# A hybrid attention trunk on one core: the third product of a unit without a follower in a PSUM bank of its own, VectorE adding the second sum to it in place of ScalarE's copy

## The chip, the core and the metric

The kernel runs on one core of one Trainium2 chip. A core has a matrix engine (TensorE, PE in the profile; PEld is its loading of weights), VectorE (DVE), ScalarE (ACT), GpSimd (POOL) and SyncE (SP), which issues most DMAs. TensorE writes only to PSUM, of which this kernel uses eight banks; VectorE and ScalarE read them out. Each engine works through its own queue in order, and waits for other engines on semaphores. The metric is device time in microseconds (us), lower is better.

## The reference

16 learned meta tokens are put ahead of 512 tokens of width 1024. Then come two layers, each with a pre-norm, a combined input projection, a branch, a SiLU gate and an output projection that is added to the stream; a final norm drops the meta tokens.

```python
def reference(x, meta, g_norm, ..., g_final):
    h = jnp.concatenate([meta, x], axis=1)              # 528 tokens x 1024, float32
    h = h + gla_branch(rmsnorm(h, g_norm[0]), ...)      # 4 heads, gated linear attention
    h = h + diff_branch(rmsnorm(h, g_norm[1]), ...)     # 8 heads, differential softmax attention
    return rmsnorm(h[:, 16:], g_final)

def gla_branch(xn, w_in, ...):
    q, k, v, z, g_lr = jnp.split(xn @ w_in, [...], axis=-1)
    ...                                  # causal, with a decay for each key channel
    return (silu(z) * head_rms(o) * gnorm) @ w_out

def diff_branch(xn, w_in, ...):
    q, k, v, z = jnp.split(xn @ w_in, 4, axis=-1)
    a = softmax(q1 k1 + bias) - lam * softmax(q2 k2 + bias)
    return (silu(z) * head_rms(a @ v) * gnorm * ...) @ w_out
```

## The kernel before

Activations lie transposed, channels on the 128 partitions and tokens along the free dimension, in two halves of 264 tokens (256 where the meta tokens are left out). Float32 accuracy is had from a faster matmul format by splitting each operand into a high part (ScalarE copies it, L276) and a low remainder (VectorE subtracts, L277): names that end in h and l, such as wh and wl. Three of the four cross products of the parts are summed.

Most input projections are done by a `Unit`: a 1024x256 block of weights is cut into quarters and multiplied with both token halves in Strassen's manner, with seven products where eight would be usual. A product is 12 matmuls into one PSUM bank (`PASSES`, L431). The banks bv and by exist once, bx twice, and a new tile named bx takes the other bx bank in turn. Sums and differences of the products become the four quarters of the result:

- The first product goes into a bx bank, and ScalarE copies it out as u (`partial`, L452; call it u1). The unit before can do this ahead of time (`nxt.first()`), so that the next starts early (`early`).
- The second product adds to the same bank, and ScalarE copies the sum out as u2.
- The third product adds to the same bank again, and ScalarE copies the sum out as u3.
- The fifth product goes into bv. VectorE makes one quarter from bv and u3 (L477), and then the sixth product adds to bv.
- The product in by and u1 make a quarter (L479), the fourth product and u3 make another (L477), and bv with u2 make the last (L479).

For a unit that was started early and has no other Unit behind it (`early and not nxt`, the only case that the change touches) TensorE's order is: second product (`p6` in the code), fifth (`p5`, bv), third (`p7`), the by product (`p2`), fourth (`p4`, bx), sixth (`p3`, bv); where `freed` is set the fourth stands right behind the third.

TensorE's order is written out by the code itself: a `Weaver` takes a few matmuls at a time from a queue of generators and places them between the steps of the attention. The other engines' queues are set by a scheduler: it takes what the code issues, by priorities (`urgent`, `soon`, `at_once`) and by its own notion of when an input will be there. So an instruction that is replaced can also reorder its neighbours on ScalarE and VectorE.

Other names that occur: in the first layer `kd` (decayed keys) is scaled on VectorE (L1218) between groups of matmuls (L1214), and `cm`, `c` are splits of those scores; `vm` is the short block of values of a head, written in three parts from a DMA's `lands` (L407 and L408 on ScalarE, L412 on VectorE) and used by L1244; L934 and L935 are a gate's tanh and its scaling, L936 the product on VectorE; `tick` is a small memset that releases the copies of v (L575); L1253 squares an output row, L972 is the output projection and L980 adds it to the stream. In the second layer `aT` and `am` are splits of transposed attention weights (L276, L277, L407, L408, L410), and L1723 multiplies `am` with the short block of values; L1740 makes a gated row `yt`, which is split into `y`.

Of the kernel before, what the change touches and what calls it, by code (L numbers as in the profile page):

```python
# [11 lines left out]
F32 = mybir.dt.float32  # L12
# [4 lines left out]
ALU = mybir.AluOpType  # L17
# [3 lines left out]
P = 128  # L21
# [7 lines left out]
HT = L // 2  # L29
# [180 lines left out]
def trunk(ctx, tc, x, meta, g_norm, gla_w_in, gla_w_gate_up, gla_b_gate, gla_gnorm, gla_w_out,  # L210
# [3 lines left out]
    act, dve, pe, pool, sp = nc.scalar, nc.vector, nc.tensor, nc.gpsimd, nc.sync  # L214
# [17 lines left out]
    def T(p, shape, dt, tag, **kw):  # L232
        uid[0] += 1
        return p.tile(shape, dt, tag=tag, name=f"{tag}_{uid[0]}", **kw)

    def pb_tile(tag):
        return T(pb_pool, [P, 512], F32, tag, bufs=2 if tag == "bx" else 1)
# [75 lines left out]
    def load(key):  # L313
        t = load_w(*key) if len(key) == 4 else load_blocks(*key)
        while behind:
            behind.pop(0)[0]()
        for i in spare.pop(key[1:], ()):
            residual_rows(i)
        return t
# [10 lines left out]
    ws = Weights(lambda *key: load(key), {"pair": 2, "sum": 1, "a11": 1, "a12": 1, "a22": 1})  # L330
# [56 lines left out]
    def want_plain(w, c0, keep=False):  # L387

        def first(raw):
            with behind_gate():  # L390
                return block_pair(raw[:, :8, :], keep)

        return ws.want((w, c0, True), [Part("pair", first),
                                       Part("pair", lambda raw: block_pair(raw[:, 8:, :]))])
# [33 lines left out]
    def product(bank, w, x, first=True):  # L428

        for i, (k, p, q) in enumerate(PASSES):  # L430
            pe.matmul(bank[:, :x[q].shape[2]], w[p][:, k * P:(k + 1) * P], x[q][:, k, :], start=first and i == 0,  # L431
                      stop=i == len(PASSES) - 1, skip_group_check=not first)
            if i % 3 == 2:
                yield 0.33

    class Unit:
# [13 lines left out]
        def partial(self):  # L450
            t = T(up[0], [P, HT], F32, "u", bufs=3)[:, :self.n]
            W.moved = act.activation(t, self.bx[:, :self.n], AF.Copy, scale=self.sc)  # L452
            return t

        def first(self):
            a11 = self.u[0]
            w = ws.use(a11)
            self.bx = pb_tile(self.tags[0])
            yield from product(self.bx, w, self.X["b11"])
            ws.done(a11)  # L460
            self.p1 = self.partial()

        def run(self):
            X, sc = self.X, self.sc
            a11, a12, a22, s21, s43 = self.u
            early = self.bx is not None
            nxt = W.following()
            nxt = nxt if isinstance(nxt, Unit) else None
            out = []

            @at_once
            def add(i, n, bank, t, sign):
                if not out:
                    out.extend(o if isinstance(o, list) else [o[:, :self.n], o[:, self.n:]] for o in self.dst())
                o, bank = out[i][n], bank[:, :self.n]
                if sign < 0:
                    W.mark = dve.scalar_tensor_tensor(o, bank, -sc, t, op0=ALU.mult, op1=ALU.subtract)  # L477
                elif sc == 1.0:
                    W.mark = dve.tensor_tensor(o, bank, t, op=ALU.add)  # L479
                else:  # L480
                    W.mark = dve.scalar_tensor_tensor(o, bank, sc, t, op0=ALU.mult, op1=ALU.add)

            def p2():
                by = pb_tile(self.tags[1])
                yield from product(by, ws.use(a12), X["b21"])
                ws.done(a12)
                add(0, 0, by, self.p1, 1)

            def p4():
                bz = pb_tile("by" if nxt else "bx")  # L490
                yield from product(bz, ws.use(a22), X["t4"])
                ws.done(a22)
                add(1, 0, bz, self.u3, -1)
                self.tail(1)

            def p5():
                self.bv = pb_tile("bv")
                yield from product(self.bv, ws.use(s21)[1], X["t1"])

            def p6():  # L500
                yield from product(self.bx, ws.use(s21)[0], X["t2"], False)
                self.u2 = self.partial()

            def p7():
                yield from product(self.bx, ws.use(s43)[1], X["t3"], False)
                self.u3 = self.partial()
                add(1, 1, self.bv, self.u3, -1)

            def p3():
                yield from product(self.bv, ws.use(s43)[0], X["b22"], False)  # L510
                ws.done(s43)
                add(0, 1, self.bv, self.u2, 1)
                self.tail(0)

            if not early:
                yield from self.first()
            before, after = {(True, True): ((p2, p5), ()), (True, False): ((p5,), (p2,)),
                             (False, True): ((p5,), ()), (False, False): ((p2,), ())}[early, nxt is not None]
            if not early:
                yield from (p2 if nxt else p5)()  # L520
            yield from p6()
            for f in before:
                yield from f()
            ws.done(s21)
            if self.freed:
                self.freed()
            yield from p7()
            if self.freed:
                yield from p4()
                self.freed()  # L530
            for f in after:
                yield from f()
            if nxt:
                yield from nxt.first()
            if not self.freed:
                yield from p4()
            yield from p3()
# [13 lines left out]
    def x_parts(i, pool=xp):  # L551
        t = T(pool, [P, 2, 4, HT], F32R, f"x{i}", bufs=1)
        return [t[:, j] for j in range(2)]

    X = {n: x_parts(i) for i, n in enumerate(("b11", "b21", "b22", "t1", "t2", "t4"))}
# [7 lines left out]
    up = [gctx.enter_context(tc.tile_pool(name="up", bufs=3))]  # L563
# [78 lines left out]
    for b in range(5):  # L642
        t0, n = BLK[b]
        t = T(gp, [P, D], F32, ("qs", "ks")[b - 1]) if b in (1, 2) else {0: z2, 3: v2[0], 4: v2[1]}[b][:, 1, :]
# [859 lines left out]
    X = {f"b{i + 1}{n + 1}": [t[:, :, n * HT:(n + 1) * HT] for t in B[i]] for i in range(2) for n in range(2)}  # L1504
# [440 lines left out]
def build(shapes):  # L1945
    import concourse.bacc as bacc

    nc = bacc.Bacc("TRN2", target_bir_lowering=False, num_devices=1, dynamic_dma_scratch_size=512)
    args = [nc.dram_tensor(f"in_{n}_dram", shp, F32, kind="ExternalInput").ap() for n, shp in shapes]
    args.append(nc.dram_tensor("out_0_dram", (1, NR, D), F32, kind="ExternalOutput").ap())  # L1950
    with tile.TileContext(nc) as tc:
        trunk(tc, *args)
    return nc
# [15 lines left out]
```

## Time and profile before

| | us |
|---|---|
| median of 3 runs | 971.44 (970.47 to 972.05) |
| the profiled execution | 970.65 |
| its span, first to last instruction | 968.9 |
| TensorE matmul busy | 957.2 |
| TensorE weight load busy | 906.9 |
| VectorE busy | 778.6 |
| ScalarE busy | 626.8 |
| GpSimd busy | 44.9 |

Busy times are of the span; those of different engines overlap. The clock that TensorE was granted was 0.999 of full speed over the span. A row of the timeline gives the start and the length in us, the engine, the line, the operation, the tile written and those read, the shape, and a count where equal instructions follow each other; a bracket tells of idle time ahead of it and what ended it. Matmuls overlap, so a row of TensorE is as long as its last matmul's modelled end; the starts within a product are 0.12 us apart.

### The profile page before, as it was taken

Reading aid. Unit: us, or ns where it says so; the run is one execution under the profiler, and the core shown is the slowest. Engines: PE = TensorE matmul, PEld = TensorE weight load, DVE = VectorE, ACT = ScalarE, POOL = GpSimd, SP = SyncE. Lnnn points to the kernel's source line nnn. Section 1 sums busy time; section 2 is a strip of 40 time slices with the busy share of each in tenths; the row PEclk is TensorE's granted clock in tenths of the full one; section 3 lists DMA queues with packets and bytes.
Section 4 is the critical chain, followed back from the end, with each engine's and each line's share of the span. In section 5 each row is a group of like instructions: output and inputs, shape, how many; then the busy total and the mean of one; then the engine's idle time right before and its main releaser. Section 6 shows DMA issues by size and latency. Waiting matters only on the chain.

```text
span 968.9 us, 18048 instructions
## 1 busy us (share of the span) xinstructions
PE 957.2 (99%) x6993; PEld 906.9 (94%) x6993; DVE 778.6 (80%) x1586; ACT 626.8 (65%) x1304; POOL 44.9 (5%) x68
## 2 busy tenths in 40 slices
PE   9999999999999999999999999999999999999997
PEld 8999999999999999998899998998999989989996
DVE  7989885886888787668997987968869769687785
ACT  7776755577647567656757776575675756755583
POOL 1000000000000000000001001000000000000001
PEclk9999999999999999999999999999999999999999
DMA  7322223635363236124355525243342341722212
GB/s 197 88 85 59 82 79 122 147 103 128 116 162 91 85 117 158 53 101 152 99 130 138 143 73 133 75 139 98 99 138 88 118 119 44 182 70 84 89 64 87
DMA packets 128522, 104.94 MB, mean 108 GB/s; under 512 B 51102, under 2 KB 112830, under 8 KB 128433
## 3 DMA queue, kind: packets, MB, share of 16 engines
q1 hardware_dynamic: 123104, 93.80, 35.1%
q10 hardware_dynamic: 5328, 9.95, 2.8%
q8 instruction: 56, 0.92, 0.4%
q14 instruction: 34, 0.27, 0.1%
HBM read 83.64 MB, written 11.80 MB: 99 GB/s over the span
## 4 chain that ended last, share of the span: by engine, by line
PE 88%; ACT 1%; DVE 1%; issue 1%; POOLq 0%; DVEq 0%
PE bx L431 19%; PE bv L431 12%; PE by L431 10%; PE bx L421 10%; PE ps L400 9%; PE bx L972 5%; PE bx L400 3%; PE bv L972 2%; PE by L972 2%; PE ps L1214 2%; PE by L400 2%; PE bv L400 2%; PE ps L1807 1%; PE bx L1807 1%; PE bv L421 1%; PE by L421 1%
## 5 line engine op out<-in xcount | busy, mean ns | idle before, releaser
L277 DVE TENSOR_TENSOR wl<-raw,wh 128x1024 fp32r<-128x1024 f32 x98 | 119.4, 1221 | 23.0 <-ACT wh L276 18.9
L276 ACT ACTIVATE wh<-raw 128x1024 fp32r<-128x1024 f32 x98 | 103.1, 1054 | 48.3 <-PE by L972 22.9
L431 PE MATMUL bv<-x,wh 128*128 128x264 f32 (+1 forms) x656 | 98.6, 287 | 0.0
L431 PE MATMUL bx<-x,wh 128*128 128x264 f32 (+1 forms) x640 | 95.6, 286 | 0.0
L431 PEld LDWEIGHTS bv<-x,wh 128*128 128x128 f32 x656 | 86.8, 189 | 0.6 <-DVE z L479 0.2
L431 PEld LDWEIGHTS bx<-x,wh 128*128 128x128 f32 x640 | 84.6, 188 | 0.7 <-ACT u L452 0.2
L452 ACT ACTIVATE u<-bx 128x264 f32<-128x264 f32 (+1 forms) x120 | 45.3, 379 | 35.5 <-PE bx L431 33.1
L1694 ACT ACTIVATE p<-p,st 128x528 f32<-128x528 f32 (+3 forms) x64 | 36.5, 570 | 41.7 <-DVE st L1692 41.4
L421 PE MATMUL bx<-x,wh 128*128 128x512 f32 (+1 forms) x256 | 62.4, 385 | 0.0
L277 DVE TENSOR_TENSOR wl<-sum,wh 128x1024 fp32r<-128x1024 f32 x41 | 50.1, 1221 | 10.6 <-ACT wh L276 10.5
L431 PE MATMUL bx<-x,wl 128*128 128x264 f32 (+1 forms) x320 | 54.1, 284 | 0.0
L431 PE MATMUL bv<-x,wl 128*128 128x264 f32 (+1 forms) x328 | 53.8, 284 | 0.1
L421 PEld LDWEIGHTS bx<-x,wh 128*128 128x128 f32 x256 | 44.4, 188 | 7.8
L276 ACT ACTIVATE wh<-sum 128x1024 fp32r<-128x1024 f32 x41 | 43.1, 1051 | 9.7 <-PE by L972 3.9
L431 PE MATMUL by<-x,a12h 128*128 128x264 f32 (+1 forms) x320 | 47.5, 286 | 0.1
L1730 POOL TENSOR_TENSOR st<-st,mhalf 128x1 f32<-128x1 f32 x32 | 25.5, 795 | 468.6 <-ACT on L1728 418.2
L431 PE MATMUL bx<-x,a11h 128*128 128x264 f32 (+1 forms) x320 | 46.6, 284 | 0.0
L431 PEld LDWEIGHTS bv<-x,wl 128*128 128x128 f32 x328 | 45.4, 188 | 0.3 <-issue 0.3
L431 PEld LDWEIGHTS bx<-x,wl 128*128 128x128 f32 x320 | 45.3, 188 | 0.3
L431 PEld LDWEIGHTS bx<-x,a11h 128*128 128x128 f32 x320 | 42.4, 188 | 0.6
L431 PEld LDWEIGHTS by<-x,a12h 128*128 128x128 f32 x320 | 42.1, 188 | 0.3 <-ACT t L1658 0.3
L276 ACT ACTIVATE a11h<-raw 128x512 fp32r<-128x512 f32 x41 | 25.7, 626 | 20.7 <-DMA raw<-in_diff_w_in_dram 7.9
(493 smaller groups left out, 2631.9 us busy)
## 6 DMA issues: line engine op xcount, KB each, us to landing
raw<-in_gla_w_in_dram SPq DMA_DIRECT2D x48, 512.0 KB, 4.5
raw<-in_diff_w_in_dram SPq DMA_DIRECT2D x42, 512.0 KB, 4.9
raw<-in_diff_w_in_dram SPq DMA_DIRECT2D x11, 1024.0 KB, 5.9
raw<-in_gla_w_out_dram SPq DMA_DIRECT2D x8, 1024.0 KB, 5.8
raw<-in_diff_w_out_dram SPq DMA_DIRECT2D x8, 1024.0 KB, 6.0
vd<-planes ACTq DMA_DIRECT2D x12, 268.0 KB, 5.8
vd<-keep ACTq DMA_DIRECT2D x12, 264.0 KB, 2.3
T<-bdr SPq DMA_DIRECT2D x8, 264.0 KB, 4.7
```

The source lines that it names most:

```text
L276: act.activation(hi, src, AF.Copy)
L277: dve.tensor_tensor(lo, src, hi.bitcast(F32), op=ALU.subtract)
L400: pe.matmul(ps, l, r, start=first and n == 0, stop=last and n == 2, **kw)
L421: pe.matmul(bank, a[:, k, :], b[k] if n0 is None else b[k][:, n0 + i * nn:n0 + (i + 1) * nn], start=n == 0 and ks[0] == 0, stop=n == len(t ...
L431: pe.matmul(bank[:, :x[q].shape[2]], w[p][:, k * P:(k + 1) * P], x[q][:, k, :], start=first and i == 0, stop=i == len(PASSES) - 1, skip_gr ...
L452: W.moved = act.activation(t, self.bx[:, :self.n], AF.Copy, scale=self.sc)
L972: pe.matmul(banks[i][:, :HT], h.t[p][:, k, mm * P:(mm + 1) * P], s.y[q][k][:, i * HT:(i + 1) * HT], start=n == 0, stop=n == len(PASSES) - 1)
L1214: pe.matmul(o, s.kd[:, i, kc], s.qs[:, i, t0:t0 + n], start=i == 0, stop=i == 1)
L1694: act.activation(p[:, :nk], p[:, :nk], AF.Exp, scale=-1.0, bias=st[:, m:m + 1], accum_out=st[:, 2 + m:3 + m])
L1730: pool.tensor_tensor(ms, ms, mhalf[:, :1], op=ALU.pow)
L1807: pe.matmul(ps[i], yp[hd][p][:, k, b * P:(b + 1) * P], wt[q][cs.start // 512][:, 2 * hd + k, cs.start % 512:(cs.stop - 1) % 512 + 1], star ...
```

## The change

In a unit that was started early and has no follower, the third product starts afresh in a new bx tile, that is in the other bx bank, and VectorE adds u2 to it while reading it out. The result takes the place of u3. All other units keep the old code. The copies of ScalarE fall from 123 to 112, eleven units being of that kind.

```diff
+        @at_once
+        def third(self, bank):
+            t = T(up[0], [P, HT], F32, "u", bufs=3)[:, :self.n]
+            if self.sc == 1.0:
+                dve.tensor_tensor(t, bank[:, :self.n], self.u2, op=ALU.add)
+            else:
+                dve.scalar_tensor_tensor(t, bank[:, :self.n], self.sc, self.u2, op0=ALU.mult, op1=ALU.add)
+            return t
+
...
             def p7():
-                yield from product(self.bx, ws.use(s43)[1], X["t3"], False)
-                self.u3 = self.partial()
+                if early and not nxt:
+                    bank = pb_tile("bx")
+                    yield from product(bank, ws.use(s43)[1], X["t3"])
+                    self.u3 = self.third(bank)
+                else:
+                    yield from product(self.bx, ws.use(s43)[1], X["t3"], False)
+                    self.u3 = self.partial()
                 add(1, 1, self.bv, self.u3, -1)
```

The order of TensorE, GpSimd and SyncE is the same as before but for the bank. On ScalarE eleven rows go, on VectorE eleven come (L459 of the changed file), and both queues are reordered at some places. Lines of the changed file stand 9 lower from L464 on and 14 lower from L521 on: L477 and L479 read L486 and L488 there, L934 and L935 read L948 and L949, L1218 reads L1232, L1253 reads L1267, L1740 reads L1754.

VectorE in the second value unit of head 2, where the two halves of kd are scaled (first layer). Before:

```order
L277 TENSOR_TENSOR wl_6122<-raw_5937,wh_6121 128x1024
L477 SCALAR_TENSOR_TENSOR t_6157<-bv_6096,u_6154 128x264
L277 TENSOR_TENSOR c_1126_6076<-ps_6103,c_1125_6075 128x128
L1218 TENSOR_SCALAR kd_5974<-kd_5974,eL_1012 128x272 x2
L479 TENSOR_TENSOR t_6156<-by_6159,u_6027 128x264
L410 TENSOR_TENSOR cm_6074<-ps_6137,cm_6074 32x128
```

And now:

```order
L277 TENSOR_TENSOR wl_6124<-raw_5939,wh_6123 128x1024
L459 TENSOR_TENSOR u_6157<-bx_6127,u_6096 128x264
L277 TENSOR_TENSOR c_1128_6078<-ps_6105,c_1127_6077 128x128
L486 SCALAR_TENSOR_TENSOR t_6160<-bv_6098,u_6157 128x264
L1232 TENSOR_SCALAR kd_5976<-kd_5976,eL_1012 128x272
L488 TENSOR_TENSOR t_6159<-by_6162,u_6029 128x264
L1232 TENSOR_SCALAR kd_5976<-kd_5976,eL_1012 128x272
L410 TENSOR_TENSOR cm_6076<-ps_6140,cm_6076 32x128
```

The new sum stands where L477 was, and the sum of the by product has moved between the two scalings of kd.

ScalarE in the second gate unit of head 3 and right behind it (first layer). Before:

```order
L452 ACTIVATE u_7723<-bx_7616 128x264
L575 ACTIVATE v_1308_7226<-keep_83,tick_7752 128x4x128 x2
L407 ACTIVATE vm_1307_7225<-lands_7602,short 32x256
L408 ACTIVATE vm_1307_7225<-lands_7602,short 32x256
L934 ACTIVATE t_7758<-t_7726 128x528
L276 ACTIVATE wh_7794<-raw_7786 128x1024
L935 ACTIVATE t_7726<-t_7726,gn_sb 128x528
L934 ACTIVATE t_7777<-t_7725 128x528
L1253 ACTIVATE t_7808,st_7809<-ps_7806 16x512
```

And now:

```order
L589 ACTIVATE v_1311_7229<-keep_83,tick_7756 128x4x128 x2
L948 ACTIVATE t_7762<-t_7730 128x528
L407 ACTIVATE vm_1310_7228<-lands_7605,short 32x256
L949 ACTIVATE t_7730<-t_7730,gn_sb 128x528
L948 ACTIVATE t_7781<-t_7729 128x528
L408 ACTIVATE vm_1310_7228<-lands_7605,short 32x256
L949 ACTIVATE t_7729<-t_7729,gn_sb 128x528
L1267 ACTIVATE t_7812,st_7813<-ps_7810 16x512
L276 ACTIVATE wh_7798<-raw_7790 128x1024
```

The gate's steps have moved ahead of the two copies that fill vm and between them, and the split of the next weights behind the squares of the output row.

VectorE in the key unit of head 3 (second layer; the keys of heads 4 to 6 are alike). Before:

```order
L1740 TENSOR_TENSOR yt_10999<-ps_10996,z_9910 128x256
L277 TENSOR_TENSOR aT_1955_10959<-ps_10952,aT_1954_10958 128x256
L410 TENSOR_TENSOR am_10957<-ps_10953,am_10957 32x128
L277 TENSOR_TENSOR y_1540_8780<-yt_10999,y_1540_8780 128x2x128
L477 SCALAR_TENSOR_TENSOR t_11017<-bv_10976,u_11012 128x264
```

And now:

```order
L1754 TENSOR_TENSOR yt_11006<-ps_11003,z_9915 128x256
L277 TENSOR_TENSOR aT_1961_10965<-ps_10958,aT_1960_10964 128x256
L459 TENSOR_TENSOR u_11019<-bx_10999,u_10980 128x264
L410 TENSOR_TENSOR am_10963<-ps_10959,am_10963 32x128
L486 SCALAR_TENSOR_TENSOR t_11024<-bv_10982,u_11019 128x264
```

The new sum, which waits for the third product, stands ahead of the split of am.

## The prediction, made before the changed kernel ran

> **What bounds the kernel now.** I read the page's busy shares and the chain that ended last, then the waits of the two TensorE rows (in the waits the columns are total us, how often, longest), then the timeline around the edited units, whose rows give start, length, engine, line, operation and, in brackets, idle time before it.
>
> ```profile
> span 968.9 us, 18048 instructions
> PE 957.2 (99%) x6993; PEld 906.9 (94%) x6993; DVE 778.6 (80%) x1586; ACT 626.8 (65%) x1304; POOL 44.9 (5%) x68
> PE 88%; ACT 1%; DVE 1%; issue 1%; POOLq 0%; DVEq 0%
> ```
>
> ```profile
> PE ps L1244 <- DVE vm L412: 0.7, 1, 0.7
> ...
> PEld bx L431 <- ACT u L452: 0.2, 1, 0.2
> ```
>
> TensorE is the bound: 957.2 of 968.9 us, and its own work is 88% of the chain. So an edit pays only if it shortens a wait of TensorE, and costs only if it lengthens or makes one. The wait that the change is about is the last row: weights for a product into bx waiting for the copy u (L452). It was long enough to see once, 0.2 us.
>
> **The change part by part.** Eleven units have no follower: in the first layer the second gate unit of head 0, the second value unit of heads 1 and 2, the second gate unit of head 3; in the second layer the key units of heads 1 to 6 and the gate unit of head 7.
>
> *The copy u3 and its substitute.* Rows of ScalarE's copy and of a VectorE sum of the same shape and operands (a PSUM bank and a u), min/median/max ns:
>
> ```profile
> L452 ACT ACTIVATE u<-bx x120: 358/379/394, 88.5 to 929.4; 128x264 f32<-128x264 f32 x99, 128x256 f32<-128x256 f32 x21
> ...
> L479 DVE TENSOR_TENSOR t<-by,u x33: 410/423/433, 141.3 to 933.3; 128x264 f32<-128x264 f32 x26, 128x256 f32<-128x256 f32 x7
> ```
>
> ScalarE loses 11 x 0.379 = 4.2 us, VectorE gains 11 x 0.423 = 4.7 us. Neither is the bound, so by themselves they are worth nothing; what counts is what each blocks in its in-order queue.
>
> *The bank of the third product.* Before, it continued in the bank of the second and had to wait until u2 was copied out. A typical key unit (head 3):
>
> ```profile
> 643.08 1.14 PE L431 MATMUL bv<-x,wh 128*128 128x264 f32 x8
> 643.96 0.37 ACT L452 ACTIVATE u<-bx 128x264 f32<-128x264 f32 x1
> 644.06 0.65 PE L431 MATMUL bv<-x,wl 128*128 128x264 f32 x4
> 644.54 0.53 PE L431 MATMUL bx<-x,wh 128*128 128x264 f32 x3
> ```
>
> The fifth product (bv) runs between second and third. The copy ended at 644.33, 0.21 us before the third product began, which began where the bv product left off (644.06 + 4 x 0.12). The 12 matmuls of bv, 1.46 us, cover the copy. Gain: 0. The 0.2 us wait of the first list lies elsewhere, in the key unit of head 7, which is not started early and so keeps the old code:
>
> ```profile
> 889.77 0.42 PEld L431 LDWEIGHTS bx<-x,wh 128*128 128x128 f32 x3 [0.22 <-ACT u L452]
> ```
>
> The fourth product then takes the bank that u2 left: free long ago, 0.
>
> [...]
>
> *Second value unit of head 2* (third product until 258.44; while it runs, the cross terms of head 2 are prepared, which scale kd between two groups of matmuls):
>
> ```profile
> 257.15 1.22 DVE L277 TENSOR_TENSOR wl<-raw,wh 128x1024 fp32r<-128x1024 f32 x1 [0.80 <-ACT wh L276]
> 258.48 0.39 ACT L452 ACTIVATE u<-bx 128x264 f32<-128x264 f32 x1
> 258.90 0.43 DVE L477 SCALAR_TENSOR_TENSOR t<-bv,u 128x264 f32<-128x264 f32 x1 [0.53 <-ACT u L452]
> 259.25 0.28 DVE L277 TENSOR_TENSOR c<-ps,c 128x128 fp32r<-128x128 f32 x1
> 259.26 0.65 PE L431 MATMUL by<-x,a12l 128*128 128x264 f32 x4
> 259.45 0.62 DVE L1218 TENSOR_SCALAR kd<-kd,eL 128x272 f32<-128x272 f32 x2
> 259.72 0.36 DVE L1218 TENSOR_SCALAR kd<-kd,eL 128x272 f32<-128x272 f32 x1
> 259.86 2.10 PE L1214 MATMUL ps<-qs,kd 128*128 128x128 f32 x16
> 259.99 0.43 DVE L479 TENSOR_TENSOR t<-by,u 128x264 f32<-128x264 f32 x1
> ```
>
> Now L479 stands between the two scalings. The new sum can start at 258.48 as the copy did; c, L477 and the first scaling follow by about 259.39, no later than before. But L479 needs the by product, whose last matmul ends at 259.26 + 0.65 = 259.91. It starts at 259.94, and behind it queue the second scaling and the split of cm. The scaling comes 0.35 later (the step from L477 to c, 258.90 to 259.25), at 260.29 and not at 259.72 (the second of the x2, shown by itself). TensorE's 16 matmuls alternate between the two halves of kd, so the third of them, 0.22 us into the group, waits for it: +0.58 us. Ends: 0.5 (L479 starts as the product ends) to 0.65 (the step is the full 0.43).
>
> [...]
>
> *Second gate unit of head 3*:
>
> ```profile
> 385.88 0.64 PE L431 MATMUL bx<-x,a22l 128*128 128x264 f32 x4
> 386.02 1.34 ACT L575 ACTIVATE v<-keep,tick 128x512 fp32r<-128x512 f32 x2 [1.71 <-DVE tick L616]
> 387.38 0.43 DVE L477 SCALAR_TENSOR_TENSOR t<-bx,u 128x264 f32<-128x264 f32 x1
> 387.83 0.43 PE L972 MATMUL bx<-y,wh 128*128 128x264 f32 x2
> 387.99 0.51 ACT L407 ACTIVATE vm<-lands,short 32x256 fp32r<-32x256 f32 x1 [0.63 <-DMA lands<-vd]
> 388.33 0.42 DVE L479 TENSOR_TENSOR t<-bv,u 128x264 f32<-128x264 f32 x1
> 388.52 0.51 ACT L408 ACTIVATE vm<-lands,short 32x256 fp32r<-32x256 f32 x1
> 388.78 0.47 DVE L412 SCALAR_TENSOR_TENSOR vm<-lands,short,vm 32x256 fp32r<-32x256 f32 x1
> 389.05 0.64 ACT L934 ACTIVATE t<-t 128x528 f32<-128x528 f32 x1
> 389.41 0.39 PE L1244 MATMUL ps<-vm,am 96*16 96x512 f32 x1 [0.67 <-DVE vm L412]
> 390.55 0.72 ACT L935 ACTIVATE t<-t,gn_sb 128x528 f32<-128x528 f32 x1
> 391.18 0.63 ACT L934 ACTIVATE t<-t 128x528 f32<-128x528 f32 x1
> ```
>
> TensorE waited here for vm, of which L407, L408 and L412 write a part each. The order now puts L934 ahead of L407, and L935 and L934 between L407 and L408. The first L934 fits into the 0.63 us in which ScalarE waited for the DMA: its input is written by L477, which moves ahead of the v remainders and starts when the fourth product ends, 385.88 + 0.64 = 386.53, so it is there at 386.99. L934 runs when the v copies let it, 387.35 to 387.99, and L407 starts at 388.02. L935 then takes a step of 0.63 (390.55 to 391.18), L934 its 0.63: L408 starts at 389.84 and ends at 390.35 instead of 389.03 (the second L934's input, L479 of 388.33, comes in time). TensorE had been released by L412's end, 389.25, so its start moves from 389.41 to 390.43: +1.02 us. Ends: 0.8 (L934 hides wholly, steps shorter) and 1.2 (full lengths 0.72 and 0.64). The next wh, now last in that stretch behind L1253, is ready about 392.7, its remainder near 394. TensorE is then still on the weights before: 48 matmuls of 0.12 us from 387.83 and the wait of 1.0 us reach 394.7, the work between them not counted. ScalarE's DMA issues and SyncE's queue keep their order.
>
> *Key units of heads 3 to 6*, where the sum stands ahead of the split of am:
>
> ```profile
> 645.66 0.41 DVE L277 TENSOR_TENSOR aT<-ps,aT 128x256 fp32r<-128x256 f32 x1
> 646.11 0.28 DVE L410 TENSOR_TENSOR am<-ps,am 32x128 fp32r<-32x128 f32 x1
> 646.42 0.39 ACT L452 ACTIVATE u<-bx 128x264 f32<-128x264 f32 x1 [0.22 <-PE bx L431]
> 647.18 0.19 PEld L1723 LDWEIGHTS ps<-vm,am 96*128 96x128 f32 x1
> ```
>
> am was ready at 646.39. The sum waits for the third product, so it starts at 646.42 like the copy, lasts 0.42, and am follows 0.03 behind its end (as it does behind aT), 646.88 to 647.16. With 0.05 from an end to a weight load that is 0.03 to 0.04 late: 4 x 0.04 = +0.15 us. Ends 0 and 0.4. Behind am wait the split of y and the next wl, both needed much later.
>
> *The other five.*
>
> ```profile
> 100.44 0.62 DVE L1218 TENSOR_SCALAR kd<-kd,eL 128x272 f32<-128x272 f32 x2
> 101.80 1.95 PE L1214 MATMUL ps<-qs,kd 128*128 128x128 f32 x16
> ...
> 532.43 0.43 DVE L477 SCALAR_TENSOR_TENSOR t<-bv,u 128x264 f32<-128x264 f32 x1 [1.23 <-ACT u L452]
> ```
>
> Head 0's gate unit: a later VectorE pushes the scaling from 100.44 to 100.7, its end to 101.3, before TensorE reads at 101.80. Head 1's value unit: the same split of the scalings, but their reader comes late enough. Keys of heads 1 and 2: VectorE idled 1.23 us for ScalarE's late copy and starts earlier now, which no TensorE wait needs. Head 7's gate: 0.35 later, taken up by VectorE's next idle time. Those gaps are the cover; without it, 0.35 each. Sum 0.
>
> Sum: 0.58 + 1.02 + 0.15 = +1.75 us, ends 1.3 and 2.25. The later stalls follow TensorE's own results, so nothing downstream takes it back. The profiled execution took 970.65 us (span 968.9), 0.8 below the median of 971.44; added to the median: 973.2.
>
> **The rivals.**
> - *Bank rotation pays* (faster). If the end of each bv product is only modelled and the third product really waited for u2, up to one copy per unit goes: 11 x 0.379 = 4.2, net -2.4, 969.0. For it: the copy ended only 0.21 us ahead in that unit. Against: no bracket stands there, and the starts are 0.12 us apart straight through. [...]
> - *The stalls are smaller* or taken up by a later wait: one or none shows, 971.4 to 972.5. For it: TensorE waits for VectorE elsewhere too, and VectorE could be ahead by then. Against: TensorE's rows later in this layer wait for what TensorE itself made.
> - *VectorE becomes the gate in the key units* (slower by over 0.2%). The sum blocks am, and then values, in four heads. If it starts 0.08 us later than the copy did, 4 x 0.08 = 0.33 us more, the sum passes 1.94 us, which is 0.2%. At 0.35 us late it is 1.4 more: 974.6. For it: by my reckoning nothing is left to spare. Against: aT ends at 646.07, so VectorE has nothing else to run when the product ends.
>
> **How the numbers follow.** About what a measurement of this kernel can tell from no change is 0.2%, 1.94 us; my sum of 1.75 lies just within. Both stalls as worked out: 0.60, of which 0.22 lands above 1.94 (bounds up to 2.25 and the spread of the runs, 970.47 to 972.05). Smaller or taken up: 0.20 (0.01 of it below the bound by a low run). VectorE the gate: 0.14. Rotation pays: 0.06. So faster 0.06 + 0.01 = 0.07, same 0.38 + 0.19 = 0.57, slower 0.22 + 0.14 = 0.36. The likeliest alone spans 972.5 to 974.0. The range goes from 971.0 (no stall shows, a low run) to 974.7 (the slower rival at its price).
>
> **What would show it.** The chain of waits afterwards: vm L1244 at 1.5 to 1.8 us; kd L1218 a second wait near 0.5 at 260; small am waits at L1723 four times; no change of the starts of third products against the bv product ahead of them. Wrong if ScalarE's first L934 is late there (then more), if L1214's third matmul doesn't stop, or if TensorE's rows shift earlier at a third product.

## The result, and the profile after

The changed kernel takes 975.32 us (median of 7 runs, 973.00 to 976.92), the kernel before 971.29 us beside it (970.47 to 972.05): ratio 1.004, 95% interval 1.0028 to 1.0053. It is slower by some 4 us where 1.75 were forecast, and lies above the range. The profiled execution took 976.17, its span is 974.1.

The page of the changed kernel, busy times:

```profile
span 974.1 us, 18053 instructions
PE 958.1 (98%) x6993; PEld 906.3 (93%) x6993; DVE 782.6 (80%) x1597; ACT 623.0 (64%) x1293; POOL 45.2 (5%) x68
```

TensorE's own work grew by 0.9 us only; VectorE got its 4.0, ScalarE lost 3.8, near the 4.7 and 4.2 that the exchange of eleven instructions should give. The other 4.3 of the 5.2 us of span are waits. TensorE's waits after (total, times, longest):

```profile
PE ps L1258 <- ACT vm L408: 1.3, 1, 1.3
...
PE ps L400 <- DVE am L410: 0.9, 1, 0.9
...
PE ps L1228 <- DVE kd L1232: 0.8, 2, 0.5
...
PE by L431 <- DVE tick L630: 0.5, 1, 0.5
```

The first and third rows were forecast. The second and the fourth were not. Since TensorE runs the same matmuls in the same order in both kernels, its n-th matmul of one can be laid beside its n-th of the other. The table gives by how much the matmuls start later than before, as the median over a stretch, and how much that grew from one stretch to the next (us):

| place (time before) | forecast | whole change, first profile | whole change, second profile |
|---|---|---|---|
| scaling of kd, head 2 (260) | +0.58 | +0.59 | +0.58 |
| next unit's first products (288 to 290) | 0 | +1.09 | +0.79 |
| vm, head 3 (389) | +1.02 | +0.60 | +0.74 |
| keys of heads 3 to 6 (645 to 840) | +0.15 | 0.03 at each am, see below | the same |
| head 7 (938) | 0 | +1.48 | +0.01 |

The second profile is the first run below (`whole_again`). What is missing to the whole difference are steps of 0.1 to 0.6 that are in one profile and not in the other. Part of them lies in the first 13 us, where the profiles of all kernels run 0.2 ahead of the profile before to 0.8 behind it, whatever was edited; they are left out below.

### The profile page after: what moved, and what is told of

The parts are those of the page before. It is cut to its first block, busy times and chain, and to the rows that moved or that the text cites. A ratio compares the mean times of both kernels' runs of the same rounds, so it can differ in the third digit from the quotient of the medians.

```text
span 974.1 us, 18053 instructions
## 1 busy us (share of the span) xinstructions
PE 958.1 (98%) x6993; PEld 906.3 (93%) x6993; DVE 782.6 (80%) x1597; ACT 623.0 (64%) x1293; POOL 45.2 (5%) x68
## 5 line engine op out<-in xcount | busy, mean ns | idle before, releaser
L452 ACT ACTIVATE u<-bx 128x264 f32<-128x264 f32 (+1 forms) x109 | 41.0, 378 | 34.5 <-PE bx L431 33.3
L421 PE MATMUL bx<-x,wh 128*128 128x512 f32 (+1 forms) x256 | 62.5, 385 | 0.0
L421 PEld LDWEIGHTS bx<-x,wh 128*128 128x128 f32 x256 | 44.5, 188 | 7.9
```

What stands on the lines that cost most here:

```text
L421: pe.matmul(bank, a[:, k, :], b[k] if n0 is None else b[k][:, n0 + i * nn:n0 + (i + 1) * nn], start=n == 0 and ks[0] == 0, stop=n == len(t ...
```

## The experiments

Units are counted in the order in which the program makes them: 3 is the second value unit of head 2, 4 the second gate unit of head 3, 5 to 10 are the keys of heads 1 to 6, 11 is the gate unit of head 7. A subset takes a counter:

```diff
-                if early and not nxt:
+                if early and not nxt and own():     # own() counts, and tells whether this unit is in the set
```

Each kernel ran beside the kernel before on the same chip. The first four shared a before of 970.76 us. Line numbers in these kernels stand some lines higher again, by what was added: with the counter alone the new sum is L465, the sums L492 and L494, the gate's tanh and scaling L954 and L955, and the sum into the stream L1000.

**The whole change again, and three subsets.** My first theory was that the wait at 289 comes from ScalarE's queue at 270, 12 us behind unit 3, and that the loss at 938 was a chance of that one run. In the changed order ScalarE takes a11h, a split that waits for a DMA, ahead of wh; the prediction does not speak of that swap. The rival took the loss at 938 for an effect of the second layer's units.

> The changed kernel once more, for a second profile. Queue theory (the value unit of head 2 lets ScalarE take a split that waits for a DMA ahead of the next weights, and TensorE waits for it at 289): median 975 (974.5 to 976), TensorE later than before by 1.0 us between 288 and 290 and by 0.5 at 260; the 1.1 to 1.4 us at 942 and the 0.5 at 810 of the first profile need not come back. Rival (the second layer's edited units cost 1.5 to 2.4 us): they come back.

> The change in the value unit of head 2 alone. Queue theory: +0.53 at 260 and +1.06 at 288 to 290, 972.9 (972.5 to 973.4), with a wider spread than before because ScalarE's wait for the DMA hangs on its landing. By the prediction's own terms: +0.58, 971.9. Rival (second layer): 972.5 at most.

> The change in the gate unit of head 3 alone. By the first profile +0.6: 971.9; by the prediction's term +1.02: 972.3. TensorE's wait for vm 1.3 to 1.75 us instead of 0.7.

> The change in nine units, without the value unit of head 2 and the gate unit of head 3. Queue theory and the prediction's terms: 971.3 to 971.6, no wait at 260, 289 or 390 beyond those of before. Rival (the second layer's units cost): 972.8 to 973.7.

| kernel | median us | ratio (95%) | TensorE's steps |
|---|---|---|---|
| whole_again | 974.16 | 1.0036 (1.0022 to 1.0050) | as above |
| only3 | 972.03 | 1.0013 (1.0004 to 1.0022) | 260: +0.59, 289: +0.96 |
| only4 | 971.38 | 1.0007 (0.9998 to 1.0016) | 389: +0.81 |
| not34 | 972.52 | 1.0018 (1.0009 to 1.0027) | 938: +1.85, else 0.1 at most |

Unit 3 causes both steps at 260 and 289. But without units 3 and 4 the kernel is still 1.76 us slower, and the step at 938 is there: the part of my theory that called it chance fell. For unit 4 the time alone is not clear of zero, the step in the trace is. Four times were misses: whole_again, only3 and only4 lie under what I gave for them, which counted from the 971.29 us of the first measurement and not from 970.76, and not34 lies above. Unit 3's time alone, 972.03, would also fit the 971.9 of the prediction's own terms; the step at 289 in its trace does not.

**Unit 3 with ScalarE's order restored.** The split a11h is queued behind the wh ahead of it, as before the change. Unit 3 itself stays as changed; on VectorE the scheduler then puts the remainders and sums of the next 15 us back into their order of before as well:

```diff
-                with tc.issue_after(W.moved.ins) if calm and b == 0 else ExitStack():
+                with (tc.issue_after(W.moved.ins) if calm and b == 0 else
+                      tc.issue_after(wh_done[-2].ins) if c0 == 4096 + 512 * 2 and b == 0 else ExitStack()):
```

> The change in the value unit of head 2 alone, with the split of the next unit's first quarter (a11h) held behind the weights' split wh on ScalarE, as before. Queue theory: 0.45 to 0.55 at 260 stays, the 0.7 to 1.06 at 288 to 290 goes: 971.3 (971.0 to 971.6). Rival (the wait at 289 comes from the scalings of kd at 260, 0.5 us late): 972.0, as with the change there alone.

971.43 us against 970.88 (1.0006, 0.9997 to 1.0015). The step at 260 is +0.59, that at 289 is +0.01: the order of these two splits, with what the scheduler makes of VectorE's queue behind them, is the cause. The timelines of the kernel before, of unit 3 alone, and of unit 3 with the order restored:

```profile
270.75 1.06 ACT L276 ACTIVATE wh<-raw 128x1024 fp32r<-128x1024 f32 x1 [3.39 <-PE by L972]
271.82 0.63 ACT L276 ACTIVATE a11h<-raw 128x512 fp32r<-128x512 f32 x1
...
279.21 1.10 SPq L298 DMA_DIRECT2D raw<-in_gla_w_in_dram  x2
...
288.50 0.42 DVE L980 TENSOR_TENSOR hT<-hT,by 128x264 f32<-128x264 f32 x1
...
289.53 1.14 PE L431 MATMUL by<-x,a12h 128*128 128x264 f32 x8
```

```profile
272.30 0.63 ACT L276 ACTIVATE a11h<-raw 128x512 fp32r<-128x512 f32 x1 [4.45 <-DMA raw<-in_gla_w_in_dram]
272.84 1.05 ACT L276 ACTIVATE wh<-raw 128x1024 fp32r<-128x1024 f32 x1
...
279.43 1.21 DVE L277 TENSOR_TENSOR wl<-raw,wh 128x1024 fp32r<-128x1024 f32 x1
280.67 0.93 SPq L298 DMA_DIRECT2D raw<-in_gla_w_in_dram  x2
...
287.58 0.69 DVE L366 TENSOR_TENSOR sum<-raw 128x512 f32<-128x512 f32 x1 [2.00 <-DMA raw<-in_gla_w_in_dram]
...
290.41 0.42 DVE L1000 TENSOR_TENSOR hT<-hT,by 128x264 f32<-128x264 f32 x1
...
290.89 1.24 PE L431 MATMUL by<-x,a12h 128*128 128x264 f32 x8 [0.50 <-DVE tick L636]
```

```profile
271.84 1.06 ACT L276 ACTIVATE wh<-raw 128x1024 fp32r<-128x1024 f32 x1 [3.41 <-PE by L994]
273.06 0.63 ACT L276 ACTIVATE a11h<-raw 128x512 fp32r<-128x512 f32 x1 [0.16 <-DMA raw<-in_gla_w_in_dram]
...
290.62 1.14 PE L433 MATMUL by<-x,a12h 128*128 128x264 f32 x8
```

How a wait of ScalarE at 272 reaches TensorE at 291 can be read downwards in the second fence. ScalarE stands before a11h until its DMA lands, and wh behind it starts at 272.84, not 270.75 (this execution lies 0.5 later as a whole here). VectorE's remainders fall behind and queue in another order; the wl that reads the raw buffer last ends at 280.64. SyncE issues the next weights into that buffer at 280.67 (before 279.21). They land later, VectorE idles 2.00 us for them, and behind that sum in its queue stands hT, which empties by. TensorE's product into by starts 0.06 behind hT's end. The bracket names tick, a memset that ends at about the same time; what the product needs by the code is the bank that hT empties. The third fence has the wh back at its place and no wait at by (that execution lies some 1.1 us later as a whole, 0.46 from its start and 0.59 from 260).

The late issue is only part of it. The second of the two loads, issued at 281.09, lands 6.37 us after its issue, where it took 4.85 in the kernel before. In all four profiles with the swap it takes 6.16 to 6.37 us, in the ten others 4.79 to 5.55. In those four a 16 KB packet of another queue, of which the next part tells, starts 3.9 to 4.2 us after the issue, inside the transfer; in the ten it starts 0.5 to 1.2 us ahead of it. From 286.2 to 286.8 the packet records of unit 3 alone hold five 1 KB packets, one after another, and nothing else; the kernel before goes straight on behind these weights with over 1000 packets of 256 bytes in a us. With 4.85 us the load would have landed at 285.9; VectorE, free at 285.58, would have idled some 0.4 us and not 2.0, and by this estimate hT would have emptied the bank by before TensorE came to it. No run moves that packet without the swap, so that it is what holds the load up is read from the records, not tried; why the swap puts it there is not shown.

**Unit 11.** It keeps all queues in their order but for the exchange of copy and sum. What else changes is a semaphore: TensorE's third product no longer waits for the copy u2; the fourth product, 12 matmuls on, does. In the records of DMA packets a 16 KB packet of the queue that the page calls "q8 instruction" stands at different places. There are 56 of them, one for every 125 matmuls or so, at the same matmuls of TensorE to within some ten in nearly all cases, and their 0.92 MB over 6993 matmuls and as many weight loads are 66 bytes each. I take them for fetches of TensorE's instructions and call them so; no view names what they carry.

> The change in the gate unit of head 7 alone. Fetch theory: without its wait for the second sum's copy TensorE's queue runs ahead, its next 16 KB of instructions are fetched about 1 us after the issue of the last output weights, ahead of their transfer, and not 4.4 us after it, behind them; the weights land 0.5 to 1.4 us later, ScalarE, GpSimd and then TensorE (at 938) wait: median 971.9 to 972.6, single runs from 970.8 to 974. Rival (VectorE's sum between the two remainders x is what delays): the fetch and the landing as before, and the same +1.1 to 1.8.

> As only11, but the third product, in its own bank and summed by VectorE, keeps TensorE's wait for the copy of the second sum. All queues in the same order as in only11. Fetch theory: fetch 4.4 us after the issue again, 970.8 (970.4 to 971.3). Rival (VectorE's sum delays): as only11, 971.9 to 972.6.

```diff
-                    yield from product(bank, ws.use(s43)[1], X["t3"])
+                    yield from product(bank, ws.use(s43)[1], X["t3"], after=W.moved)
...
+            if after is not None and i == 0:
+                tc.add_manual_dep(mm.ins, after.ins.name, mybir.DependencyInfo(
+                    mybir.DependencyClass.Sync, mybir.DependencyReason.DATA), reason="moved")
```

Against 970.88, unit 11 alone takes 972.39 (1.0019, 1.0010 to 1.0027), with the wait restored 971.09 (1.0000, 0.9991 to 1.0009). The step at 938 is +1.44 and +0.01. Unit 11 alone, timeline and the wait it ends in:

```profile
925.50 0.37 SPq L285 DMA_DIRECT2D raw<-in_diff_w_out_dram  x1
...
931.58 1.06 ACT L276 ACTIVATE x<-raw 128x1024 fp32r<-128x1024 f32 x1 [2.00 <-DMA raw<-in_diff_w_out_dram]
...
934.15 1.22 DVE L277 TENSOR_TENSOR x<-raw,x 128x1024 fp32r<-128x1024 f32 x1
934.18 1.60 POOL L1750 TENSOR_TENSOR st<-st,mhalf 128x1 f32<-128x1 f32 x1 [31.64 <-ACT on L1748]
935.81 0.47 ACT L1751 ACTIVATE on<-ps,st 128x256 f32<-128x256 f32 x1 [1.24 <-POOL st L1750]
...
939.64 0.56 PE L400 MATMUL ps<-k,q 128*128 128x144 f32 x3 [0.94 <-DVE am L410]
```

The same with the wait restored:

```profile
925.90 0.37 SPq L285 DMA_DIRECT2D raw<-in_diff_w_out_dram  x1
...
930.99 1.06 ACT L276 ACTIVATE x<-raw 128x1024 fp32r<-128x1024 f32 x1 [1.01 <-DMA raw<-in_diff_w_out_dram]
...
933.58 0.68 POOL L1753 TENSOR_TENSOR st<-st,mhalf 128x1 f32<-128x1 f32 x1 [30.64 <-ACT on L1751]
934.30 0.48 ACT L1754 ACTIVATE on<-ps,st 128x256 f32<-128x256 f32 x1 [0.32 <-POOL st L1753]
...
939.15 1.31 PE L400 MATMUL ps<-y,aT 128*128 128x256 f32 x9
```

And the DMA queues in 0.2 us from 926.5 (unit 11 alone), then in 0.3 us from 930.2 (wait restored), with packets, MB and the time of the packets as a share of 16 engines' time (over 100% where packets run on beyond so short a window):

```profile
q1 hardware_dynamic: 11, 0.02, 225.8%
q8 instruction: 1, 0.02, 43.3%
```

```profile
q8 instruction: 1, 0.02, 21.9%
q1 hardware_dynamic: 21, 0.02, 16.4%
```

The last output weights (1 MB) begin to move 1.04 us after their issue in both. Without the wait the fetch begins 1.06 us after the issue, together with them; with the wait, 4.44 us after it, when they are nearly through. All fourteen profiles at this place, from the packet records and timelines:

| kernel | fetch after issue, us | weights used by ScalarE after issue | GpSimd's st | step at 938 |
|---|---|---|---|---|
| the ten others (unit 11 not edited, or with the wait) | 4.32 to 4.64 | 5.06 to 5.27 | 0.55 to 0.71 | 0.01 at most |
| whole_again | 0.80 | 5.52 | 0.55 | +0.01 |
| whole change, only11 | 0.98, 1.06 | 6.12, 6.08 | 1.60 | +1.48, +1.44 |
| not34 | 1.10 | 6.49 | 1.60 | +1.85 |

With the fetch ahead of the transfer, or beside its start, the weights land 0.25 to 1.4 us later. The packet records show how. In the ten, the last 2 KB packet of the weights starts 4.46 to 4.64 us after the issue, and from 2 to 4.25 us some 200 start in each us. In the four it starts at 4.91 (whole_again), 5.47, 5.51 and 5.88 (not34), and the last of them go one after another: 12 in 1 us in not34, which is 6.4% of the time of 16 engines, about one engine's. In the whole change 13 of them, 0.084 to 0.093 us long, start from 4.53 to 5.51 us, one every 0.08 us. I read this as one of the sixteen fallen behind while the rest are done. That it is the one with the fetch fits, but the records do not name the engine. In the three late ones a second thing adds to it: GpSimd's st, 0.55 to 0.71 us long otherwise, now starts 0.02 to 0.03 us after VectorE's remainder x of 1.22 us and takes 1.60, ending 0.41 after it. The kernel before has the same: eight of its st rows begin 0.42 to 0.92 us into such a remainder of 1.22 us, last 0.70 to 1.21 and end 0.41 behind it; rows that begin while VectorE is idle or works from a PSUM bank last 0.54 to 0.55. In whole_again it starts 0.10 ahead of that remainder and takes 0.55, and TensorE loses nothing. Behind st stand ScalarE's on, aT and am, for which TensorE waits. The rival (the sum itself delays) is out, since with the wait restored the sum is there and the loss is not.

That the removed wait lets TensorE's sequencer run ahead, and so ask for its instructions earlier, is my explanation, which no row shows; shown is that restoring the wait moves the fetch back, and the loss goes with it. A second place fits it: in all seven kernels whose key units are changed, one other fetch, near the key unit of head 5 (at 770 to 773 us), comes some 40 matmuls of TensorE earlier than in the seven whose are not, and there it costs nothing that the steps show.

**The first ten units, and the other eight.**

> The change in the first ten units. If the three places add up: 970.8 + 1.3 (head 2) + 0.6 (head 3) = 972.7 (972.2 to 973.2), nothing after 400 us. If the key units cost as well (0.2 to 0.5): 973.0.

972.62 against 970.88 (1.0019, 1.0010 to 1.0027); steps +0.59, +1.09 and +0.63, nothing at 938. The three places add up.

> The change in the eight units that are left: head 0's gate, head 1's values, the keys of heads 1 to 6. If the three other places are all there is: as before, 970.9 (970.5 to 971.3). If the key units' sums ahead of the split of am cost, as the prediction had it: 971.1 (0.15 us more); as its slower rival had it, 972 and above.

971.07 against 970.75 (1.0003, 0.9994 to 1.0012). No step of 0.1 us or more that unit 1, 2 or a key unit would explain; at the keys the steps are 0.03 to 0.05. The time alone cannot tell the first of the three expectations from the second; it rules out the third.

**Unit 4 with vm first.** A priority for vm's parts in head 3 puts L407 and L408 ahead of the tanh again:

```diff
-                split3(s.vm[:, 256 * h:256 * h + 256], pm, 32, short[:, NM:NM + 1])
+                with tc.high_priority(offset=40) if (hd, h) == (3, 1) else ExitStack():
+                    split3(s.vm[:, 256 * h:256 * h + 256], pm, 32, short[:, NM:NM + 1])
```

> The change in the gate unit of head 3 alone, the three parts of vm given a priority that puts both of ScalarE's ahead of the gate's tanh again. If the queue order at vm is the cause: wait for vm 0.7 us again, 970.9 (970.5 to 971.2). If the new sum itself delays the chain: 971.4, as without the priority.

970.44 against 970.75 (0.9998, 0.9988 to 1.0007); the wait for vm is 0.5 us, not the 0.7 expected, the step at 389 is -0.21. The order at vm was the cause. The 0.2 us are a small gain that the change does bring: VectorE's sum L477 (L492 here) no longer stands between the two remainders of v but ahead of them, in idle time, so that L412, for which TensorE waits, starts 0.24 us earlier (388.73 less the 0.19 by which this execution lies later here, against 388.78).

**All eleven units, mended.** The three mends together; then a fourth, by which head 2's by sum gets a lower priority and stands behind both scalings of kd:

```diff
-            @at_once
             def add(i, n, bank, t, sign):
+                low = lone[0] == 3 and (i, n) == (0, 0) and early and not nxt     # lone[0]: own()'s count
+                urgent(add_now, 60 if low else 160)(i, n, bank, t, sign)
+
+            def add_now(i, n, bank, t, sign):
```

> The change in all eleven units with three mends: a11h behind wh (head 2), vm ahead of the tanh (head 3), TensorE's wait for the copy kept in head 7's gate unit. What is left by the theory is the 0.45 to 0.55 us at 260 (the scaling of kd): 971.4 (971.1 to 971.8), no wait at 289, 389 or 938 beyond those of before. If the change gains anything by itself, it must show here: below 970.8.

> The change in all eleven units with the three mends and a fourth: in head 2 the sum of the by product stands behind both scalings of kd on VectorE again. By the prediction's term for head 2 (0.58; 0.45 to 0.55 measured) the wait at 260 goes: as before, 970.8 (970.4 to 971.3), and nothing of the change is left, for better or worse. If the banks gain anything once nothing stands against it: below 970.3.

971.54 against 970.75 (1.0005, 0.9995 to 1.0014), with the step of +0.58 at 260 left; and 970.86 against 970.58 (1.0002, 0.9993 to 1.0011), with none left. In both the step at 389 is -0.21 to -0.23. Once nothing stands against it, no gain or loss is left that these runs can tell; the interval goes from 0.7 us faster to 1.1 us slower, and the 0.2 us at vm are lost in it.

## Why the prediction was wrong

The sum failed at two places that it put at nothing, and both are steps of the argument: that unit 3 costs nothing behind 260 (0.8 to 1.1 us were lost at 289), and that head 7's gate unit is taken up by idle time (1.4 to 1.9 us were lost at 938). The two stalls that it did name together came out a little smaller than forecast. Two of its side sums are off by 0.1 at most (4 x 0.08 is 0.32, and 387.83 + 48 x 0.12 + 1.0 is 394.6), which changes nothing.

*What bounds the kernel* was right: TensorE has 98% of the span, and 4.3 of the 5.2 us lost are its waits.

*Bank of the third product, gain 0*: right for TensorE's time. Key unit of head 3 in the changed kernel:

```profile
646.68 0.65 PE L431 MATMUL bv<-x,wl 128*128 128x264 f32 x4
...
647.17 0.53 PE L431 MATMUL bx<-x,wh 128*128 128x264 f32 x3
...
649.05 0.43 DVE L459 TENSOR_TENSOR u<-bx,u 128x264 f32<-128x264 f32 x1 [0.34 <-PE bx L431]
...
649.51 0.28 DVE L410 TENSOR_TENSOR am<-ps,am 32x128 fp32r<-32x128 f32 x1
649.85 0.19 PEld L1737 LDWEIGHTS ps<-vm,am 96*128 96x128 f32 x1
```

The third product begins 0.49 us after the start of the last four matmuls of bv, 0.48 before. all_mended shows no gain of that size either, so the first rival (net -2.4 us) fell. But the removed wait was not worth nothing: with it gone, the fetch in head 7's gate unit starts 1.06 us after the issue of the weights (unit 11 alone) and not 4.44.

*Second value unit of head 2, +0.58*: +0.58 to +0.59 measured in every kernel that has it, by the mechanism told. Unit 3 alone, 0.09 us early as a whole here:

```profile
258.39 0.43 DVE L465 TENSOR_TENSOR u<-bx,u 128x264 f32<-128x264 f32 x1
...
259.28 0.35 DVE L1238 TENSOR_SCALAR kd<-kd,eL 128x272 f32<-128x272 f32 x1
259.85 0.43 DVE L494 TENSOR_TENSOR t<-by,u 128x264 f32<-128x264 f32 x1 [0.22 <-PE by L431]
260.20 0.35 DVE L1238 TENSOR_SCALAR kd<-kd,eL 128x272 f32<-128x272 f32 x1
```

```profile
259.78 0.46 PE L1234 MATMUL ps<-qs,kd 128*128 128x128 f32 x2
260.61 1.60 PE L1234 MATMUL ps<-qs,kd 128*128 128x128 f32 x12 [0.37 <-DVE kd L1238]
```

The sum of the by product and the second scaling start at 259.94 and 260.29 when the 0.09 is added, as forecast, and TensorE stops at the third matmul. The step that failed is that the unit's cost ended there. The text ahead of the prediction shows three places at which queues are reordered; a fourth, ScalarE's swap of wh and a11h, 12 us behind the unit, is in neither, and it cost another 0.8 to 1.1 us.

*Second gate unit of head 3, +1.02*: the mechanism was right, the size too large. Unit 4 alone:

```profile
387.20 0.63 ACT L954 ACTIVATE t<-t 128x528 f32<-128x528 f32 x1
387.88 0.51 ACT L407 ACTIVATE vm<-lands,short 32x256 fp32r<-32x256 f32 x1
388.30 0.72 ACT L955 ACTIVATE t<-t,gn_sb 128x528 f32<-128x528 f32 x1
388.93 0.63 ACT L954 ACTIVATE t<-t 128x528 f32<-128x528 f32 x1
389.58 0.51 ACT L408 ACTIVATE vm<-lands,short 32x256 fp32r<-32x256 f32 x1
...
390.14 0.40 PE L1264 MATMUL ps<-vm,am 96*16 96x512 f32 x1 [1.48 <-ACT vm L408]
```

L408 starts 1.70 us after L407; the forecast had 1.82 (388.02 to 389.84), 0.12 more, nearly all of it in the step from L407 to the scaling: 0.42 us (387.88 to 388.30), where L407 to L408 had been 0.53 before. L407 started 0.08 earlier than forecast (387.88 is 387.94 when this execution's start, 0.06 early, is taken out; the forecast was 388.02). That is the 0.2 by which +0.81 falls short of +1.02. In the whole change, where all runs 2 us later, it is 0.60 to 0.74; what takes the rest there stays open.

*Key units, +0.15*: right. The split of am starts 0.46 behind the sum, and TensorE's matmul behind it is 0.03 late, as worked out (2.63 us later than before ahead of it, 2.66 behind). The slower rival, VectorE as the gate there, fell.

*The other five, 0*: this failed. Head 7's gate was to be 0.35 later and be taken up by idle time. With TensorE's wait restored, VectorE did take it up (step +0.01). The loss of 1.4 to 1.9 us came by a way that is in none of the rivals: the weights landed up to 1.4 us late behind a fetch, and GpSimd's st, begun 0.02 to 0.03 us into VectorE's remainder, took 1.60 us instead of 0.55 to 0.71. It does not come in every execution; whole_again's profile has the early fetch and no loss.

The terms as measured by medians against the before beside them: unit 3 +1.27, unit 4 +0.62, unit 11 +1.51, in all 3.40; the whole change, beside the same before as the first two, +3.40. In the first measurement it was +4.03. That the sum fits to 0.01 is luck, since single runs of the whole change lie between 973.00 and 976.92.

## What to carry to other kernels

Where a scheduler sets the queues, go through every place at which the order differs, to the end of the program: the largest miss on an order was two swapped splits 12 us behind the edit, of which one waits for a DMA. Look at the DMA packets too: in both places that the forecast missed, a 16 KB packet of the instruction queue had come to lie at the weights' transfer. In a kernel whose bound engine waits for 1% of its time, an edit that moves other engines' work by 0.4 us has more to lose than to gain (here 3.40 us against 0.2), and a wait that costs its engine nothing can still be what keeps something else in its place (here the fetch in head 7's gate unit). When a version is slower by a fraction of a per cent, splitting the edit by place and laying the bound engine's n-th instruction of both kernels side by side shows each loss as a step.

## What the runs showed of the hardware

At the two places where a 16 KB packet, by my reading a fetch of TensorE's instructions, had moved into a transfer of weights or just ahead of it, the weights landed late: begun 0.8 to 1.1 us after their issue, 1 MB was used at 5.52 to 6.49 us after it instead of 5.06 to 5.27; begun 3.9 to 4.2 us after the issue, 512 KB landed at 6.16 to 6.37 us instead of 4.79 to 5.55. The end of these transfers went one packet after another: 13 of 2 KB from 4.53 to 5.51 us after the issue in the whole change, five of 1 KB in 0.6 us in unit 3 alone. I read this as the share of one DMA engine.

A GpSimd operation of 0.55 us took 1.60 where a VectorE subtraction of two SBUF operands (1.22 us) had started 0.02 to 0.03 us earlier, and ended 0.41 behind it; where such a subtraction had started 0.42 to 0.92 us earlier it took 0.70 to 1.21, with the same 0.41.

In the kernel before, a matmul of 512 columns whose operands are float32 (L1441) shows as two rows of 0.59 us, and the next matmul starts 0.95 us after the first of them (454.01 to 454.96); behind one on split parts (L421) the next starts after 0.23 us (453.56 to 453.79).
